# Index rows and one-hots of a token router: one broadcast row and every second one-hot of the first coefficient build move to TensorE and ScalarE

## The chip, the cores and the metric

The kernel runs on one core of a Trainium2 chip. The metric is the device time of one launch in microseconds (us); the time given for a kernel is the median of its runs. Engines are called TensorE (PE in the profile), VectorE (DVE), ScalarE (ACT), GpSimd (POOL) and SyncE (SP, which only issues transfers here).

## The reference, cut to what matters

The network is one hybrid layer; the part that matters is its last block, PEER: 8 heads pick 16 experts each for every token, out of 128 x 128.

```python
idx = ...                                   # (tokens, 128): index = i1 * 128 + i2, 16 for each of 8 heads
u   = jnp.take(u_tab, it, axis=0)           # one 2048-long row per pick
act = jax.nn.gelu(jnp.einsum("td,tkd->tk", xt, u))
v   = jnp.take(v_tab, it, axis=0)
out = jnp.einsum("tk,tkd->td", gt * act, v)
```

There are 256 tokens, in two tiles of 128 (tile 0 and tile 1), and 128 picks ("slots") per token.

## The kernel before, in words

The dot product of a token with a picked row is split by columns. The last 1280 columns are gathered: `dot` fetches one row per token for one slot (GpSimd, an indirect transfer into one of five `u` buffers) and VectorE multiplies it with the token and sums (L861). The first 768 columns are done densely: `dense` multiplies all 16384 rows with all tokens on TensorE and leaves the products in `W[0]` (tile 0) and `W[1]` (tile 1).

Then the picked products have to be taken out of `W`. This is `settle`, which runs beside the last gathered dots. For each of 32 groups of 4 tokens, `extract` loads the two index rows of the group's 4 x 128 picks, broadcast to all 128 partitions (`ids`, L906; the first index is row 0, the second row 1). From row 1 ScalarE makes a one-hot E (Abs with the partition number as bias, L908, then Relu, L909). TensorE multiplies `W` with it (`y`, L912). `pick` then compares row 0 with the partition number on VectorE and multiplies with y (`hit`, L920), and TensorE sums over the partitions (`more`, L922). `ids` lies in one of five places of 512 columns in tensors that are free by then (`id_at`: two in `hnF`, three in `hnT`); a place is loaded again when its `hit` is done.

After the 32 groups of tile 0 come those of tile 1, and between them `build` for tile 0: for each group of 4 tokens VectorE makes two one-hots R and L (L929), R is scaled by the coefficients (four scalings of 128 columns, L936 on ScalarE or L938 on VectorE, as the string `R_BY` says), TensorE multiplies them (`pw`, L939), and ScalarE copies the result into `W` (L940), which now holds a dense matrix of coefficients. When all dots and picks are done, 32 builds for tile 1 follow without other work beside them. The last stage multiplies the coefficients with all rows of the second table.

The order of VectorE's work is written out by hand: each dot is one tick, and 2.4 steps of `settle` are laid behind each tick. Other engines get their order from a scheduler. The picks start in the row behind tick 185:

```python
R_BY = ('AAAA', 'AVAV')                      # L68: scalings of a build: A = ScalarE, V = VectorE
for n in range(groups + LAG):                # settle, LAG = 2
    if n < groups: held[n] = extract(routes[tt], n)
    if n >= LAG:   pick(routes[tt], n - LAG, *held[n - LAG])
    if tt and n < groups: build(routes[0], n, R_BY[0], "ut", 2)
```

E has two buffers. R, L and `hit` share four (tag "raw"), and `pw` of the first builds uses two PSUM buffers (tag "ut").

Of the kernel before, what the change touches and what calls it, by code (L numbers as in the profile page):

```python
# [9 lines left out]
F32 = mybir.dt.float32  # L10
F32R = mybir.dt.float32r
BF16 = mybir.dt.bfloat16
I32 = mybir.dt.int32
U32 = mybir.dt.uint32
AF = mybir.ActivationFunctionType
ALU = mybir.AluOpType
# [4 lines left out]
P = 128  # L21
T = 256
NTT = T // P
# [15 lines left out]
NSLOT = PH * TOPK  # L39
# [7 lines left out]
KD = 6  # L47
# [17 lines left out]
SETTLE_RATE = 2.4  # L65
SETTLE_AT = 185
LAG = 2
R_BY = ('AAAA', 'AVAV')  # L68


@with_exitstack
def trunk(ctx, tc, a, out, dbg=None):
    nc = tc.nc
    V, S, G, PE, SY = nc.vector, nc.scalar, nc.gpsimd, nc.tensor, nc.sync

    def bc(ap, shape):
        return ap.to_broadcast(shape)
# [3 lines left out]
    dram = ctx.enter_context(tc.tile_pool(name="dram", bufs=1, space=DRAM))  # L81
# [7 lines left out]
    iota = consts.tile([P, T], F32, name="iota")  # L89
# [3 lines left out]
    identb = consts.tile([P, P], BF16, name="identb")  # L93
    V.tensor_copy(identb, ident)
    part = consts.tile([P, 2], F32, name="part")
# [25 lines left out]
    with ExitStack() as wctx:  # L121
        atx = wctx.enter_context(ExitStack())
        wp = wctx.enter_context(tc.tile_pool(name="wp", bufs=3, side="right"))
        at = atx.enter_context(tc.tile_pool(name="at", bufs=1))
# [71 lines left out]
        with ExitStack() as mctx:  # L196
# [165 lines left out]
            for i, nm in enumerate(("ssm_c_re", "ssm_c_im")):  # L362
# [3 lines left out]
                for w in range(2):  # L366
                    V.tensor_scalar(cbd[:, :, w, :], craw, par[:, w:w + 1], -1.0 if i else 1.0, op0=ALU.mult,
                                    op1=ALU.mult)
# [192 lines left out]
            for k in range(CW):  # L561
                for q in range(CQ):
                    src = cpad[:, q, k:k + T]
                    if k == 0:
                        V.tensor_scalar(acc[:, q, :], src, cwT[:, q, 0:1], colv[:, 0, q:q + 1], op0=ALU.mult,
                                        op1=ALU.add)
                    else:
                        V.scalar_tensor_tensor(acc[:, q, :], src, cwT[:, q, k:k + 1], acc[:, q, :],  # L568
                                               op0=ALU.mult, op1=ALU.add)
# [4 lines left out]
            for q in range(CQ):  # L574
                S.activation(acc[:, q, :], acc[:, q, :], AF.Silu, bias=colv[:, 2, q:q + 1],
                             scale=colv[:, 1, q:q + 1])
# [122 lines left out]
        rt = uctx.enter_context(tc.tile_pool(name="rt", bufs=1))  # L699
        up = uctx.enter_context(tc.tile_pool(name="up", bufs=1))  # L700
        gp = uctx.enter_context(tc.tile_pool(name="gp", bufs=GATHER_BUFS))
        hnF = up.tile([P, NTT, DG], F32, name="hnF")
        hnT = up.tile([P, KD, T], F32, name="hnT")
# [29 lines left out]
        for tt in range(NTT):  # L733
            V.tensor_scalar(dg[:, tt, :], ident, r8[:, tt:tt + 1], None, op0=ALU.mult)
            PE.matmul(pr[:, tt * P:(tt + 1) * P], ones, dg[:, tt, :], start=tt == 0, stop=tt == 1,
                      skip_group_check=True)
# [12 lines left out]
    class Route:  # L749
# [70 lines left out]
        def gates(self):  # L820
            self.gate = gate = rt.tile([P, PH, TOPK], F32, name="gate", bufs=2)
            gs = rt.tile([P, 2, PH], F32, name="gs")
            V.tensor_sub(gate, self.tm, bc(self.tm[:, :, 0:1], [P, PH, TOPK]))
            S.activation(gate, gate, AF.Exp)
            ib = rt.tile([P, 2, NSLOT], BF16, name="ib")
            S.copy(ib, self.II.rearrange("p s h k -> p s (h k)"))
            for i in range(4):
                SY.dma_start(ib_dram[self.tt][:, i], ib[i * NQ:(i + 1) * NQ].rearrange("n s k -> n (s k)"))
            for _ in range(6):
                yield  # L830
            V.tensor_reduce(gs[:, 0], gate, axis=AX.X, op=ALU.add)
            V.reciprocal(gs[:, 1], gs[:, 0])
            V.tensor_mul(gate, gate, bc(gs[:, 1, :, None], [P, PH, TOPK]))
            V.tensor_scalar(vidx[self.tt], self.uidx.rearrange("p h k -> p (h k)"), float((DC - DU) // GU), None,
                            op0=ALU.add)
            pt = psu.tile([P, 2, P], F32, name="ptc", tag="pw", bufs=1)
            for i in range(2):
                PE.transpose(pt[:, i, :], self.II[:, i].rearrange("p h k -> p (h k)"), ident)
            self.tr = lr_p.tile([P, 2, P], F32, name="tr", bufs=2)
            S.copy(self.tr, pt)  # L840
            yield
# [14 lines left out]
        def dot(self, j):  # L856
# [5 lines left out]
                                   accum_out=self.act[:, j:j + 1])  # L862

    NQ = P // 4
    id_at = [x.bitcast(BF16).rearrange("p (i s k) -> p i s k", i=4, s=2) for x in
             [hnF[:, 0, n * 512:(n + 1) * 512] for n in range(2)]
             + [hnT.rearrange("p k t -> p (k t)")[:, n * 512:(n + 1) * 512] for n in range(KD // 2)]]
    ib_dram = [dram.tile([NQ, 4, 2 * NSLOT], BF16, name=f"ib_dram{tt}") for tt in range(NTT)]
    coef = [consts.tile([P, NSLOT], F32, name=f"coef{tt}") for tt in range(NTT)]
    vidx = [consts.tile([P, NSLOT], I32, name=f"vidx{tt}") for tt in range(NTT)]  # L870
    wa_p = ctx.enter_context(tc.tile_pool(name="wa_p", bufs=1, side="right", reuse_waits="tile"))
# [1 line left out]
    lr_p = lr_x.enter_context(tc.tile_pool(name="lr_p", bufs=2, side="right", reuse_waits="tile"))  # L873
    psx = ctx.enter_context(ExitStack())
    psu = psx.enter_context(tc.tile_pool(name="psu", bufs=2, space=PSUM))
# [6 lines left out]
    def dense():  # L882
        for b in range(NB):
# [17 lines left out]
                S.copy(W[1][:, b - 1:b + 1, :], ps[:, :, P:])  # L901
            yield

    def extract(route, g):
        ids = id_at[(route.tt * NQ + g) % len(id_at)]
        SY.dma_start(ids.rearrange("p i s k -> p i (s k)"), ib_dram[route.tt][g:g + 1].to_broadcast([P, 4, 2 * NSLOT]))  # L906
        E = lr_p.tile([P, 4, P], F32, name="E", tag="ut", bufs=2)
        S.activation(E, ids[:, :, 1, :], AF.Abs, bias=part[:, 1:2], scale=1.0)  # L908
        S.activation(E, E, AF.Relu, bias=1.0, scale=-1.0)  # L909
        y = psu.tile([P, 4, P], F32, name="y", tag=("sy", "sy", "pw")[g % 3], bufs=(2, 2, 1)[g % 3])  # L910
        for i in range(4):
            PE.matmul(y[:, i, :], W[1][:, :, i * NQ + g] if route.tt else W[0][:, i * NQ + g, :], E[:, i, :], start=i == 0, stop=i == 3,  # L912
                      skip_group_check=True)
        return ids, y

    def pick(route, g, ids, y):
        if g == 0:
            route.more = psu.tile([P, NSLOT], F32, name="more", bufs=1)
        hit = lr_p.tile([P, 4, P], F32, name="hit", tag="raw", bufs=4)
        V.scalar_tensor_tensor(hit, ids[:, :, 0, :], part[:, 0:1], y, op0=ALU.is_equal, op1=ALU.mult)  # L920
        for i in range(4):
            PE.matmul(route.more[i * NQ:(i + 1) * NQ, :], onecol[:, NQ - g:2 * NQ - g], hit[:, i, :], start=g == 0,  # L922
                      stop=g == NQ - 1)

    def build(route, g, by, tag, bufs):
        ts = slice(4 * g, 4 * g + 4)
        LR = [lr_p.tile([P, 4, P], F32, name=nm, tag="raw", bufs=4) for nm in "RL"]
        for x, at in zip(LR, (0, 1)):
            V.tensor_tensor(x, bc(iota[:, None, :P], [P, 4, P]), bc(route.tr[:, at, ts, None], [P, 4, P]),  # L929
                            op=ALU.is_equal)  # L930
        R, L = LR
        pw = psu.tile([P, 4, P], F32, name="pw", tag=tag, bufs=bufs)
        for i in range(4):
            c = route.cT[:, 4 * g + i:4 * g + i + 1]
            if by[i] == "A":
                S.activation(R[:, i, :], R[:, i, :], AF.Copy, scale=c)  # L936
            else:
                V.tensor_scalar(R[:, i, :], R[:, i, :], c, None, op0=ALU.mult)  # L938
            PE.matmul(pw[:, i, :], L[:, i, :], R[:, i, :], start=i == 0, stop=i == 3, skip_group_check=True)  # L939
        S.copy(W[route.tt][:, :, ts], pw.rearrange("p t b -> p b t"))  # L940
# [29 lines left out]
    def settle():  # L970
        groups = P // 4
        for tt in range(NTT):
            held = {}
            for n in range(groups + LAG):
                if n < groups:
                    held[n] = extract(routes[tt], n)
                    yield
                if n >= LAG:
                    pick(routes[tt], n - LAG, *held[n - LAG])
                    yield  # L980
                if tt and n < groups:
                    build(routes[0], n, R_BY[0], "ut", 2)
                    yield
            if tt == 0:
                while tick[0] <= NSLOT:
                    yield
                yield from routes[0].finish()
# [10 lines left out]
    for tt in range(NTT):  # L998
        for g in range(len(GROUPS[tt])):
            while (tt, g) not in ready:  # L1000
                next(routing)
            h0, n = routes[tt].heads(g)
# [13 lines left out]
    for g in range(P // 4):  # L1016
        build(routes[1], g, R_BY[1], ("sy", "ut")[g % 2], 2)
    uctx.close()
# [68 lines left out]
    for tt, st in enumerate(sts):  # L1087
        for c, cs_ in enumerate([slice(DC, D)] + COLS):
# [4 lines left out]
            else:  # L1093
                V.scalar_tensor_tensor(sq[tt][:, cs_], src, st[:, NCH + 2:NCH + 3], gF[:, cs_], op0=ALU.mult,
                                       op1=ALU.mult)
# [30 lines left out]
```

## Time and profile before

| what | value |
|---|---|
| median of 3 runs | 2144.23 us (2141.84 to 2145.15) |
| the profiled execution: its time, its span | 2139.49 us, 2137.6 us |
| busy share of the span | PE 92%, DVE 83%, ACT 47%, POOL 34% |
| picks of tile 0 (first `hit` to the last) | 1340.8 to 1413.2 us |
| picks of tile 1 with the builds of tile 0 | 1417.8 to 1545.7 us |
| builds of tile 1 | 1549.9 to 1602.3 us |

The shares are averages over all stages. A stage is read from its own window: which engine is busy through it, and who waits for whom.

### The profile page before, as it was taken

What the parts mean: (1) busy time and instruction counts of PE and PEld (TensorE: products, weight loads), DVE (VectorE), ACT (ScalarE), POOL (GpSimd) and SP (SyncE); (2) the same over time, 40 slices, a digit from 0 to 9 for tenths busy, and PEclk for the clock granted to TensorE, in tenths of its full rate; (3) what the DMA queues carried; (4) which work ended last, traced back from release to release, by engine and by line L of the source; (5) the groups of instructions that cost most, each with busy time, mean ns of one, the idle gap of its engine ahead of it and who ended that gap; (6) DMA issues with size and microseconds to landing.
All of it is one profiled execution on the core that took longest, in us unless ns stands there. A gap on an engine that the chain in (4) does not pass through costs nothing.

```text
span 2137.6 us, 31790 instructions
## 1 busy us (share of the span) xinstructions
PE 1970.1 (92%) x11459; PEld 1699.6 (80%) x11459; DVE 1776.7 (83%) x2903; ACT 1002.5 (47%) x1681; POOL 736.9 (34%) x546
## 2 busy tenths in 40 slices
PE   8998888999999999899999998689779999999997
PEld 7987786677799888788878886567667888888886
DVE  6789999987665557999976666889998899899997
ACT  5764444446444445233333333467673444444444
POOL 0000000000000003444455666433207777677773
PEclk9999899999999999999999999789899999999998
DMA  7554444554965567789999999988619999999995
GB/s 251 161 180 151 127 150 133 163 172 148 313 204 169 166 201 275 268 308 343 319 345 401 404 408 380 363 315 273 204 68 314 359 350 339 343 337 340 340 338 197
DMA packets 199132, 567.59 MB, mean 266 GB/s; under 512 B 31537, under 2 KB 36513, under 8 KB 198848
## 3 DMA queue, kind: packets, MB, share of 16 engines
q1 hardware_dynamic: 141632, 322.27, 45.7%
q0 software_dynamic: 57344, 243.30, 30.2%
q8 instruction: 90, 1.47, 0.3%
q14 instruction: 66, 0.54, 0.1%
HBM read 553.57 MB, written 11.93 MB: 265 GB/s over the span
## 4 chain that ended last, share of the span: by engine, by line
PE 47%; DVE 23%; issue 12%; DMA 9%; POOL 6%; ACT 3%; SPq 0%; POOLq 0%; DVEq 0%; ACTq 0%
PE acc L1073 8%; PE acc L1074 8%; PE acc L1072 8%; POOL u L859 5%; DVE u L861 5%; PE mm L183 4%; PE mm L181 4%; PE mm L182 4%; DVE acc L568 3%; DVE w_lo L163 3%; DMA hnT<-ib_dram 2%; PE mm L173 2%; PE mm L174 2%; PE mm L172 2%; DMA hnF<-ib_dram 1%
## 5 line engine op out<-in xcount | busy, mean ns | idle before, releaser
L861 DVE SCALAR_TENSOR_TENSOR u<-u,hnF 128x1280 f32<-128x1280 f32 x256 | 388.5, 1520 | 86.5 <-DMA u<-in_peer_u,uidx 84.9
L1037 POOL DMA_INDIRECT v<-in_peer_v,vidx x256 | 383.8, 1499 | 190.2 <-ACT WB L940 68.8
L859 POOL DMA_INDIRECT u<-in_peer_u,uidx x256 | 311.2, 1216 | 338.7 <-DVE u L861 262.9
L162 ACT CAST w_hi<-w_raw 128x1024 fp32r<-128x1024 f32 (+2 forms) x228 | 231.4, 1017 | 289.7 <-PE mm L182 125.0
L163 DVE TENSOR_TENSOR w_lo<-w_raw,w_hi 128x1024 fp32r<-128x1024 f32 (+2 forms) x228 | 277.2, 1219 | 106.9 <-ACT w_hi L162 103.1
L897 PE MATMUL sy<-hnT,ut 128*128 128x256 f32 x1536 | 356.8, 385 | 9.3 <-ACT ut L893 9.3
L897 PEld LDWEIGHTS sy<-hnT,ut 128*128 128x128 f32 x1536 | 287.1, 193 | 50.5 <-ACT ut L893 15.1
L103 ACT CAST vh<-vr 128x1472 fp32r<-128x1472 f32 x128 | 183.2, 1431 | 263.6 <-PE acc L1073 263.6
L1073 PE MATMUL acc<-vh,wl 128*128 128x512 f32 (+1 forms) x768 | 296.9, 387 | 3.6 <-DVE wl L1063 3.6
L183 PE MATMUL mm<-aT_hi,w_lo 128*128 128x256 f32 x960 | 274.3, 295 | 26.7 <-DVE w_lo L163 26.5
L1074 PE MATMUL acc<-vl,wh 128*128 128x512 f32 (+1 forms) x768 | 295.2, 386 | 0.0
L742 POOL TENSOR_TENSOR hnT<-aT_hi,aT_lo 128x1024 f32<-128x1024 f32 (+1 forms) x2 | 3.8, 1904 | 812.9 <-ACT w_hi L162 812.9
L181 PE MATMUL mm<-aT_hi,w_hi 128*128 128x256 f32 x960 | 279.8, 294 | 3.7 <-DVE sg L264 2.3
L1072 PE MATMUL acc<-vh,wh 128*128 128x512 f32 (+1 forms) x768 | 277.1, 385 | 2.7 <-ACT vh L103 2.2
L182 PE MATMUL mm<-aT_lo,w_hi 128*128 128x256 f32 x960 | 276.9, 291 | 0.0
L104 DVE TENSOR_TENSOR vl<-vr,vh 128x1472 fp32r<-128x1472 f32 x128 | 216.6, 1692 | 38.3 <-ACT vh L103 38.0
L1039 DVE SCALAR_TENSOR_TENSOR accg<-v,coef,accg 128x576 f32<-128x576 f32 x256 | 208.9, 816 | 11.9 <-DMA v<-in_peer_v,vidx 8.1
L183 PEld LDWEIGHTS mm<-aT_hi,w_lo 128*128 128x128 f32 x960 | 186.4, 198 | 34.3 <-DVE w_lo L163 30.6
L181 PEld LDWEIGHTS mm<-aT_hi,w_hi 128*128 128x128 f32 x960 | 189.3, 198 | 7.8 <-DVE sg L264 2.5
L182 PEld LDWEIGHTS mm<-aT_lo,w_hi 128*128 128x128 f32 x960 | 189.8, 198 | 1.3 <-issue 0.4
L893 ACT COPY ut<-ut 128x768 f32<-128x768 f32 x128 | 100.3, 801 | 165.6 <-PE ut L891 163.1
L1073 PEld LDWEIGHTS acc<-vh,wl 128*128 128x128 f32 x768 | 145.2, 189 | 35.0 <-DVE wl L1063 4.7
(333 smaller groups left out, 3362.7 us busy)
## 6 DMA issues: line engine op xcount, KB each, us to landing
vr<-in_peer_v SPq DMA_DIRECT2D x128, 736.0 KB, 6.7
raw<-in_peer_u SPq DMA_DIRECT2D x128, 384.0 KB, 6.4
w_raw<-in_w_kv_mem SPq DMA_DIRECT2D x64, 512.0 KB, 3.8
w_raw<-in_w_in SPq DMA_DIRECT2D x48, 512.0 KB, 4.0
w_raw<-in_w_out SPq DMA_DIRECT2D x32, 512.0 KB, 5.4
w_raw<-in_w_q_mem SPq DMA_DIRECT2D x32, 512.0 KB, 4.3
w_raw<-in_w_o_mem SPq DMA_DIRECT2D x32, 512.0 KB, 4.6
hnT<-ib_dram SPq DMA_DIRECT2D x38, 256.0 KB, 5.8
```

What stands on the lines that cost most here:

```text
L162: S.copy(hi, raw)
L163: V.tensor_sub(lo, raw, hi.bitcast(F32))
L181: PE.matmul(o, wh, ah, start=first and cb % 2 == 0, stop=False, skip_group_check=True)
L182: PE.matmul(o, wh, al, start=False, stop=False, skip_group_check=True)
L183: PE.matmul(o, wl, ah, start=False, stop=last and end, skip_group_check=True)
L859: G.indirect_dma_start(out=u, out_offset=None, in_=a["peer_u"].rearrange("e (q c) -> (e q) c", c=GU), in_offset=bass.IndirectOffsetOnAxis( ...
L861: V.scalar_tensor_tensor(u, u, 1.0, hnF[:, self.tt, :], op0=ALU.mult, op1=ALU.mult, accum_out=self.act[:, j:j + 1])
L897: PE.matmul(ps[:, b % 2, :], ut[:, k, :], hnT[:, k, :], start=k == 0 and b % 2 == 0, stop=k == KD - 1 and b % 2 == 1, skip_group_check=True)
L1037: G.indirect_dma_start(out=v, out_offset=None, in_=table, in_offset=bass.IndirectOffsetOnAxis(ap=vidx[tt][:, j:j + 1], axis=0))
L1072: PE.matmul(o, wh[:, tt, :], vh[:, cs_], start=b == 0, stop=False)
L1073: PE.matmul(o, wl[:, tt, :], vh[:, cs_], start=False, stop=False)
L1074: PE.matmul(o, wh[:, tt, :], vl[:, cs_], start=False, stop=b == NB - 1)
```

## The change: what it does

Three things are changed.

- Tile 0's `extract` loads only index row 0. Row 1 is put on all partitions by TensorE: four matmuls whose weights are one column of the identity, broadcast, and whose moving operand is `ib` (the bf16 index rows, now kept). ScalarE reads the result from PSUM (`pb`). A place is half as wide for tile 0, so there are eleven instead of five; tile 1 has five as before.
- In the builds of tile 0 every second group (g odd, `far`) gets its one-hot R from two bf16 matmuls into PSUM (`df`: index minus column number), and ScalarE's Abs and Relu; L stays on VectorE.
- In the builds of tile 1 ScalarE does three of the four scalings and VectorE one (`AAVA`).

```diff
-R_BY = ('AAAA', 'AVAV')
+R_BY = ('AAAA', 'AAVA')
...
-            ib = rt.tile([P, 2, NSLOT], BF16, name="ib")
+            self.ib = ib = rt.tile([P, 2, NSLOT], BF16, name="ib", bufs=2)
...
+    def id_tiles(ns):
+        n = ns * 2 * P
+        room = [hnF[:, 0, :], hnT.rearrange("p k t -> p (k t)")]
+        return [x[:, i:i + n].bitcast(BF16).rearrange("p (s i k) -> p s i k", i=4, s=ns) for x in room
+                for i in range(0, x.shape[1] - n + 1, n)]
+
+    id_at = [id_tiles(1), id_tiles(2)]
...
+    row0 = lr_p.tile([P, P], BF16, name="row0", bufs=1)
+    G.memset(row0, 0.0)
+    G.memset(row0[0:1, :], 1.0)
+    falling = lr_p.tile([P, P], BF16, name="falling", bufs=1)
+    S.activation(falling, iota[:, :P], AF.Copy, scale=-1.0)
...
-        S.activation(E, ids[:, :, 1, :], AF.Abs, bias=part[:, 1:2], scale=1.0)
+        if route.tt:
+            at = ids[:, 1]
+        else:
+            at = psu.tile([P, 4, P], F32, name="pb", tag="ut")
+            for i in range(4):
+                t = i * NQ + g
+                PE.matmul(at[:, i, :], bc(identb[:, t:t + 1], [P, P]), route.ib[:, 1, :], start=i == 0, stop=i == 3,
+                          skip_group_check=True)
+        S.activation(E, at, AF.Abs, bias=part[:, 1:2], scale=1.0)
...
-        for x, at in zip(LR, (0, 1)):
+        far = route.tt == 0 and g % 2 == 1
+        if far:
+            df = psu.tile([P, 4, P], F32, name="df", tag="ut")
+            PE.matmul(df, route.ib[:, 0, :], bc(identb[:, ts, None], [P, 4, P]), start=True, stop=False)
+            PE.matmul(df, row0, bc(falling[:, None, :], [P, 4, P]), start=False, stop=True)
+            S.activation(LR[0], df, AF.Abs)
+            S.activation(LR[0], LR[0], AF.Relu, bias=1.0, scale=-1.0)
+        for x, at in list(zip(LR, (0, 1)))[far:]:
```

How the instructions stand now, at three places. On SP's queue the index loads of tile 0 (`ib_dram_8319`) stood, before, in runs of two and three; `hnF` and `hnT` are the tensors in which the places lie:

```order
L906 DMA hnF<-ib_dram_8319 128x1024 x2
L906 DMA hnT<-ib_dram_8319 128x1024 x3
L906 DMA hnF<-ib_dram_8319 128x1024 x2
L906 DMA hnT<-ib_dram_8319 128x1024 x3
L906 DMA hnF<-ib_dram_8319 128x1024 x2
```

In the change they stand in runs of five and six at half the width, and the first two-row loads of tile 1 (`ib_dram_8320`) follow:

```order
L917 DMA hnF<-ib_dram_8319 128x512 x5
L917 DMA hnT<-ib_dram_8319 128x512 x6
L917 DMA hnF<-ib_dram_8319 128x512 x5
L917 DMA hnT<-ib_dram_8319 128x512 x6
L917 DMA hnF<-ib_dram_8319 128x512 x5
L917 DMA hnT<-ib_dram_8319 128x512 x5
L917 DMA hnF<-ib_dram_8320 128x1024 x2
L917 DMA hnT<-ib_dram_8320 128x1024 x3
```

The load of a place thus stands eleven groups ahead of its use instead of five.

On ScalarE, in the middle of tile 1's picks, two builds of tile 0 stood like this before (E: the one-hot of a pick, R: a build's scalings, WA: the copy of a finished build):

```order
L936 ACTIVATE R<-R,cT 128x128 x4
L908 ACTIVATE E<-hnT,part 128x512
L909 ACTIVATE E<-E 128x512
L936 ACTIVATE R<-R,cT 128x128 x4
L908 ACTIVATE E<-hnF,part 128x512
L940 COPY WA<-pw 128x128x4
L909 ACTIVATE E<-E 128x512
L940 COPY WA<-pw 128x128x4
```

In the change, for two builds of which the first is `far`:

```order
L953 ACTIVATE R<-df 128x512
L928 ACTIVATE E<-hnF,part 128x512
L954 ACTIVATE R<-R 128x512
L929 ACTIVATE E<-E 128x512
L963 ACTIVATE R<-R,cT 128x128 x4
L928 ACTIVATE E<-hnF,part 128x512
L929 ACTIVATE E<-E 128x512
L963 ACTIVATE R<-R,cT 128x128 x4
L967 COPY WA<-pw 128x128x4
L928 ACTIVATE E<-hnT,part 128x512
L967 COPY WA<-pw 128x128x4
```

The Abs and Relu of R are new, and between them and the copy that frees a PSUM buffer stand two E that wait for index loads.

On TensorE, at the same place, before:

```order
L922 MATMUL more<-hit,onecol 32x128 x4
L912 MATMUL y<-E,WB 128x128 x4
L939 MATMUL pw<-R,L 128x128 x4
L922 MATMUL more<-hit,onecol 32x128 x4
L912 MATMUL y<-E,WB 128x128 x4
L939 MATMUL pw<-R,L 128x128 x4
```

and in the change:

```order
L951 MATMUL df<-identb,ib 128x512
L952 LDWEIGHTS row_8338
L952 MATMUL df<-falling,row_8338 128x512
L942 MATMUL more<-hit,onecol 32x128 x4
L932 MATMUL y<-E,WB 128x128 x4
L942 MATMUL more<-hit,onecol 32x128 x4
L932 MATMUL y<-E,WB 128x128 x4
L966 MATMUL pw<-R,L 128x128 x8
```

The matmuls of two builds now stand together behind two y, and the `df` of the next pair directly behind them.

## Rows read from the trace of the kernel before

**Rows 1.** Busy time by stage (windows); PEclk is TensorE's granted clock, then DMA share, GB/s.

```profile
core 0: us, PE busy (x) PEld busy (x) DVE busy (x) ACT busy (x) POOL busy (x), PEclk, DMA share, GB/s
1340.80:1413.20 72.40, 54.76 (x488) 40.99 (x489) 59.50 (x87) 37.61 (x57) 28.05 (x27) 0.81 0.97 357
...
1417.80:1545.70 127.90, 112.00 (x757) 96.93 (x755) 118.92 (x181) 92.36 (x218) 39.01 (x38) 0.94 0.76 253
...
1549.90:1602.30 52.40, 38.08 (x256) 33.26 (x256) 49.02 (x124) 37.56 (x97) 0.00 (x0) 0.95 0.20 70
1602.30:2120.00 517.70, 512.08 (x2289) 432.69 (x2290) 465.21 (x640) 234.24 (x386) 383.75 (x256) 0.99 0.92 332
```

**Rows 2.** Waits, 1340.8 to 1413.2: total us, times, longest.

```profile
ACT E L908 <- DMA hnF<-ib_dram: 20.9, 10, 13.0
...
ACT E L908 <- DMA hnT<-ib_dram: 13.6, 12, 1.9
DVE hit L920 <- PE y L912: 11.0, 15, 2.8
...
DVE u L861 <- DMA u<-in_peer_u,uidx: 1.8, 2, 1.6
```

**Rows 3.** Transfers, 1340.8 to 1413.2: queues; issues, size, us to landing.

```profile
q0 software_dynamic: 3960, 18.02, 65.3%
q1 hardware_dynamic: 4253, 7.76, 31.6%
...
hnT<-ib_dram SPq DMA_DIRECT2D x18, 256.0 KB, 7.3
...
u<-in_peer_u,uidx POOLq DMA_INDIRECT x27, 7.7
```

**Rows 4.** TensorE in order of time (start, us), second stage, where nothing stalls it.

```profile
1447.85 0.43 PE L922 MATMUL more<-hit,onecol 128*32 128x128 f32 x8
1448.20 2.02 PE L912 MATMUL y<-E,WB 128*128 128x128 f32 x8
1450.05 1.06 PE L939 MATMUL pw<-R,L 128*128 128x128 f32 x8
1451.04 0.43 PE L922 MATMUL more<-hit,onecol 128*32 128x128 f32 x8
```

**Rows 5.** VectorE in order of time, second stage.

```profile
1535.98 0.69 DVE L929 TENSOR_TENSOR L<-iota,tr 128x512 f32<-128x512 f32 x1
1536.58 1.49 DVE L861 SCALAR_TENSOR_TENSOR u<-u,hnF 128x1280 f32<-128x1280 f32 x1
...
1537.99 0.75 DVE L920 SCALAR_TENSOR_TENSOR hit<-hnF,part,y 128x512 f32<-128x512 bf16 x1
```

**Rows 6.** ScalarE's groups, 1417.8 to 1545.7: busy, mean ns, idle before.

```profile
L936 ACT ACTIVATE R<-R,cT 128x128 f32<-128x128 f32 x128 | 40.6, 389 | 0.5 <-DVE R L929 0.5
L940 ACT COPY WA<-pw 128x512 f32<-128x512 f32 x32 | 18.6, 582 | 15.8 <-PE pw L939 15.4
L909 ACT ACTIVATE E<-E 128x512 f32<-128x512 f32 x29 | 18.2, 626 | 0.4
L908 ACT ACTIVATE E<-hnT,part 128x512 f32<-128x512 bf16 x17 | 12.3, 722 | 9.9 <-DMA hnT<-ib_dram 9.8
L908 ACT ACTIVATE E<-hnF,part 128x512 f32<-128x512 bf16 x12 | 8.7, 721 | 6.7 <-DMA hnF<-ib_dram 5.1 <-PE y L912 1.6
```

**Rows 7.** VectorE and ScalarE in order of time, builds of tile 1.

```profile
1562.38 0.68 DVE L929 TENSOR_TENSOR R<-iota,tr 128x512 f32<-128x512 f32 x1
...
1563.10 0.69 ACT L936 ACTIVATE R<-R,cT 128x128 f32<-128x128 f32 x2 [0.43 <-DVE R L929]
1563.59 0.48 DVE L938 TENSOR_SCALAR R<-R,cT 128x128 f32<-128x128 f32 x2
1563.70 0.56 ACT L940 COPY WB<-pw 128x512 f32<-128x512 f32 x1
...
1563.98 0.69 DVE L929 TENSOR_TENSOR R<-iota,tr 128x512 f32<-128x512 f32 x1
...
1564.70 0.69 ACT L936 ACTIVATE R<-R,cT 128x128 f32<-128x128 f32 x2 [0.44 <-DVE R L929]
```

More of the change, by code (lines that the diff above doesn't have):

```diff
@@ L824, in gates @@
             S.activation(gate, gate, AF.Exp)
-            ib = rt.tile([P, 2, NSLOT], BF16, name="ib")
+            self.ib = ib = rt.tile([P, 2, NSLOT], BF16, name="ib", bufs=2)
             S.copy(ib, self.II.rearrange("p s h k -> p s (h k)"))
             for i in range(4):
-                SY.dma_start(ib_dram[self.tt][:, i], ib[i * NQ:(i + 1) * NQ].rearrange("n s k -> n (s k)"))
+                SY.dma_start(ib_dram[self.tt][:, :, i], ib[i * NQ:(i + 1) * NQ])
             for _ in range(6):
@@ L864, in trunk @@
     NQ = P // 4
[L865 to L868, printed above, removed]
+    def id_tiles(ns):
[4 more added lines that the diff above has]
+    id_at = [id_tiles(1), id_tiles(2)]
+    ib_dram = [dram.tile([NQ, 2, 4, NSLOT], BF16, name=f"ib_dram{tt}") for tt in range(NTT)]
     coef = [consts.tile([P, NSLOT], F32, name=f"coef{tt}") for tt in range(NTT)]
@@ L902, in dense @@
             yield
+    row0 = lr_p.tile([P, P], BF16, name="row0", bufs=1)
[3 more added lines that the diff above has]
+    S.activation(falling, iota[:, :P], AF.Copy, scale=-1.0)
     def extract(route, g):
-        ids = id_at[(route.tt * NQ + g) % len(id_at)]
-        SY.dma_start(ids.rearrange("p i s k -> p i (s k)"), ib_dram[route.tt][g:g + 1].to_broadcast([P, 4, 2 * NSLOT]))
+        ids = id_at[route.tt][g % len(id_at[route.tt])]
+        ns = 1 + route.tt
+        SY.dma_start(ids.rearrange("p s i k -> p s (i k)"),
+                     ib_dram[route.tt][g:g + 1, :ns].rearrange("n s i k -> n s (i k)").to_broadcast([P, ns, 4 * NSLOT]))
         E = lr_p.tile([P, 4, P], F32, name="E", tag="ut", bufs=2)
-        S.activation(E, ids[:, :, 1, :], AF.Abs, bias=part[:, 1:2], scale=1.0)
+        if route.tt:
[7 more added lines that the diff above has]
+        S.activation(E, at, AF.Abs, bias=part[:, 1:2], scale=1.0)
         S.activation(E, E, AF.Relu, bias=1.0, scale=-1.0)
@@ L919, in pick @@
         hit = lr_p.tile([P, 4, P], F32, name="hit", tag="raw", bufs=4)
-        V.scalar_tensor_tensor(hit, ids[:, :, 0, :], part[:, 0:1], y, op0=ALU.is_equal, op1=ALU.mult)
+        V.scalar_tensor_tensor(hit, ids[:, 0], part[:, 0:1], y, op0=ALU.is_equal, op1=ALU.mult)
         for i in range(4):
```

## The prediction

> **What bounds the kernel now.** I read the busy time by stage first, since the shares over the whole span mix stages. Three stages are touched, and the last one, the product with the second table, is not: there TensorE is busy 512.1 of 517.7 us, and it can't start before the builds of tile 1 are done, since each of its products needs coefficients of all tokens [rows 1]. So every microsecond by which the builds end earlier or later moves the end of the kernel by as much.
>
> First stage, picks of tile 0: 72.4 us. VectorE is busy for 59.5 of it, while the transfers have a share of 0.97 and TensorE's granted clock is 0.81, a mix of its two levels [rows 1]. The waits tell the order of things: VectorE waits 11.0 us for y, and ScalarE, which makes the one-hot that y needs, waits 20.9 + 13.6 = 34.5 us for index rows [rows 2]. These are 256 KB each and land 7.3 us after issue, in the middle of 27 gathers [rows 3]. The index rows end last here.
>
> Second stage, picks of tile 1 and builds of tile 0: 127.9 us, VectorE 118.9, TensorE 112.0, ScalarE 92.4 [rows 1]. VectorE bounds it, with 9.0 us of idle time.
>
> Third stage, builds of tile 1: one build every 1.60 us (from R to R), and VectorE runs without a gap while ScalarE stands idle for 0.44 us of each [rows 7].
>
> **First stage, priced.** Removed: ScalarE's wait for index rows, and half the bytes of 32 broadcasts. Moved: the loads stand eleven places ahead, and only `hit` needs them. Three things can bound the stage afterwards.
> - VectorE: 59.5 us, unchanged [rows 1].
> - Transfers: the gathers' queue took 65.3% of the 16 engines' time, 47.3 us; the other 31.6%, 22.9 us, for 7.76 MB, which is 30 broadcasts of 262 KB or 0.77 us each [rows 3]. Of tile 0's 32 rows 11 now land before the first `hit`; 21 remain, and I count four of tile 1's. A half row costs 0.38 us if bytes set the price, 0.77 if the number of packets does (it stays at 128). So 47.3 + 4 x 0.77 + 21 x 0.38 to 0.77 = 58.4 to 66.6 us.
> - TensorE: the new `pb` are four loads of weights and four matmuls of 128 columns a group. No bf16 matmul of this shape is in the trace. Above stands half of a `pw` of 8 instructions with 128-column weights (from 1450.05 to 1451.04: 0.99, half is 0.5), below half of a `more` with 32-column weights (0.35, half is 0.18) [rows 4]; I take 0.4, since the weights are as wide as those of `pw`. 32 x 0.4 = 13 us. At the clock of 0.81 that makes 54.8 + 13 / 0.81 = 70.8 us; if the clock rises to the second stage's 0.94 [rows 1], 54.8 x 0.81 / 0.94 + 13 / 0.94 = 61 us. It should rise, since TensorE has fewer waits, but not at once.
>
> I take 65 us, the middle of TensorE's two cases: 7.4 us gained. The bounds are 61 (VectorE's 59.5 and its 1.8 us of waits for gathers [rows 2]) and 70.8, so 11.4 to 1.6. What is late next is y, by TensorE instead of by the index rows.
>
> **Second stage, priced.** VectorE loses 16 one-hots of 0.60 us each (L to the next instruction, 1535.98 to 1536.58 [rows 5]): 118.9 - 9.6 = 109.3. ScalarE gains 16 times an Abs out of PSUM and a Relu. The nearest rows are a copy out of PSUM of the same size (0.58), the Abs of E (0.72) and its Relu (0.63) [rows 6]: between 1.21 and 1.35 for both; I take 1.2, since neighbours overlap by a little: 92.4 + 19.2 = 111.6. TensorE gains 16 `df`, two matmuls of 512 columns with two loads of weights. They stream 1024 columns as a `more` does (0.35 for eight times 128), and at most cost as a `pw` (0.99) [rows 4]; I take 0.5, nearer to the first, since there are two loads of weights instead of eight. TensorE's own cycle without stalls is 3.19 us (more to more, 1447.85 to 1451.04 [rows 4]): 32 x 3.19 + 8 = 110.
>
> So three engines come to 109 to 112 us each where one had 119. In a chain of in-order queues that feed each other, equal loads cost more waiting, not less: on ScalarE each E that waits for its index row now holds up the Abs, Relu and scalings behind it, for which `pw` waits on TensorE. Before, the longest engine had 9.0 us of idle time; I add a third and take 12: 124 us, 3.9 gained. The bounds are 116 (half of the idle time, all else hidden) and 136 (the third rival): 11.9 gained to 8.3 lost.
>
> **Third stage, priced.** ScalarE has two scalings (0.30 us apart, 0.69 for both), the copy, and the gap. One more scaling of 0.30 fits into the gap of 0.44, so ScalarE comes to 1.60 - 0.44 + 0.30 = 1.46; VectorE loses one of two scalings that take 0.39 (1563.59 to 1563.98): 1.60 - 0.19 = 1.41 [rows 7]. The period becomes 1.46: 32 x 0.14 = 4.5 us. The first builds are paced by the coefficients' arrival, so I take 4.0, with bounds of 3 and 5.
>
> **At nothing:** `row0` and `falling` are made once, beside the dense loop, in which ScalarE and GpSimd wait; exposed they would cost under 1 us (a 128-column ScalarE instruction takes 0.39 [rows 6]). The writes of `ib_dram` are as many as before and are read much later.
>
> **Sum.** 7.4 + 3.9 + 4.0 = 15.3. The profiled execution took 2139.5 us, 4.7 below the median of the runs shown; the same difference on the median gives 2144.2 - 15.3 = 2129 us.
>
> **Rivals.**
> 1. The first stage stays bound by transfers or by TensorE's low clock. For it: a share of 0.97 and a clock of 0.81 [rows 1]. Against it: fewer bytes. 70.8 us there: 1.6 + 3.9 + 4.0 = 9.5 gained, 2135 us. The Trainium skill (DMA: Bandwidth & Descriptors, Specifications) gives 512 B as the smallest transfer at line rate, so rows of 1 KB should cost by their bytes; no run here shows such a row yet.
> 2. The second stage follows VectorE after all, 116 us: 7.4 + 11.9 + 4.0 = 23.3, 2121 us. For it: ScalarE had 33.3 us idle there, the sum of its groups' idle times [rows 6].
> 3. `df` takes a PSUM buffer that is free only when ScalarE has copied a `pw`, and that copy stands behind E's that wait for index rows, 9.9 + 6.7 = 16.6 us in the stage [rows 6]. Half of that falls into the stretch of a `far` build; if it comes on top, the stage takes 127.9 + 8.3 = 136 us, and 7.4 - 8.3 + 4.0 = 3.1 gained: 2141 us, no change that can be measured.
> 4. Slower: ScalarE's queue becomes the chain of the second stage. If its waits stay as they are, since they are waits for others (92.4 + 33.3 = 125.7 [rows 1, 6]), and each `far` adds its full 1.35, the stage takes 125.7 + 21.6 = 147 us, 19.4 more; with the other two terms 8.0 lost, 2152 us. It decides from 1.0 us uncovered per `far` build ((11.4 + 4.3) / 16). Against it: 15.4 us of these waits are for `pw`, which waits for R, and would shrink with it. The one-hot takes ScalarE about twice VectorE's time (1.35 against 0.69 [rows 5, 6]). That is the rule of the Trainium skill (ScalarE: Activation LUTs, Rules for kernel authors): Relu and its like belong on VectorE, not on ScalarE. Here the trace agrees on the price of one instruction; by the rule alone the move would cost time.
>
> **How the numbers follow.** My forecast 0.55, rival 1 0.15, rival 2 0.12, rival 3 0.11, rival 4 0.07. 0.2% (4.3 us) is about what a measurement of this kernel tells from no change. Forecast and rivals 1 and 2 are faster: 0.82; rival 3 the same: 0.11; rival 4 slower: 0.07. The range leaves out the last two, 0.18: it goes from 2117 (all three terms near their best: 11.4 + 11.9 + 4.0 = 27) to 2140.
>
> **What would show it.** E of tile 0 no longer waits for any transfer; its first stage takes about 65 us with TensorE's clock above 0.81 (70 and a DMA share near 1: rival 1). The second stage takes about 124 us with ScalarE busy about 111; idle time before `df` and behind E's waits would speak for rival 3, ScalarE without gaps for rival 4. The builds of tile 1 come every 1.46 us. I am wrong if the second stage grows by more than 11 us, or if the last stage takes longer than its 518 us.

## The result

The changed kernel takes 2124.52 us (median of 4 runs, 2121.98 to 2127.19), the kernel before 2144.23: a ratio of 0.9915, with a 95% interval of 0.9899 to 0.993. That is 19.7 us less where 15.3 were forecast. The profiled execution took 2121.98 us (span 2120.0), 17.5 less than that of before. One kernel further down (`hit`'s buffers alone) had two slow runs among its five, 3160.74 and 3809.32 us, which stand in no ratio here.

Busy time by stage after the change (windows; columns as in [rows 1]): picks of tile 0, picks of tile 1 with builds of tile 0, builds of tile 1, and the last stage.

```profile
1342.30:1402.80 60.50, 53.41 (x597) 41.99 (x597) 58.24 (x87) 39.60 (x59) 25.75 (x28) 0.96 0.97 363
...
1406.40:1532.60 126.20, 113.85 (x784) 94.57 (x784) 110.00 (x163) 106.81 (x250) 39.08 (x38) 0.97 0.78 258
...
1536.80:1583.50 46.70, 37.74 (x256) 32.84 (x256) 42.66 (x92) 45.26 (x130) 0.34 (x1) 0.95 0.23 78
1583.50:2102.00 518.50, 511.56 (x2287) 432.48 (x2288) 465.61 (x640) 234.17 (x387) 385.36 (x256) 0.99 0.93 332
```

Against [rows 1] the first stage is 11.9 us shorter (7.4 forecast), the second 1.7 (3.9), the third 5.7 (4.0). The last stage lasts as long as before, within 1 us. The first `hit` came 1.5 us later: over the fourteen executions profiled here it lies anywhere from 1337.5 to 1347.9 us, in the ten with half-size rows from 1341.7 on, in the four others up to 1341.9. The 1.5 us are there already at the first gathered dot, some 500 us earlier (844.4 us before, 845.9 after; 843.1 to 851.3 over the fourteen); whether the rest of the spread belongs to the half rows stays open. So the length of a stage says more than one run's total.

**First stage.** Waits of the changed kernel, 1342.3 to 1402.8 (total us, times, longest), to be read beside [rows 2]:

```profile
ACT E L928 <- PE y L932: 29.1, 24, 15.7
...
DVE u L861 <- DMA u<-in_peer_u,uidx: 1.5, 3, 0.5
```

E's waits for index rows, 34.5 us, are gone, and so are VectorE's 11.0 for y. ScalarE's 29.1 us are harmless: it is ahead and waits until y has read an older E. VectorE is busy for 58.24 of the 60.50 us, so the stage now lasts as long as VectorE's own work. The transfers of the same stretch, beside [rows 3] (packets, MB, share of 16 engines):

```profile
q0 software_dynamic: 4010, 18.26, 77.0%
q1 hardware_dynamic: 3495, 3.62, 19.4%
```

The engines are as full as before (0.97), since the stage shrank as its transfers did: the index rows take 11.7 us of the 16 engines where they took 22.9, the gathers 46.6 where they took 47.3. VectorE hardly waits for them (1.5 us above), so the transfers are close behind VectorE and do not end last. TensorE's clock, cut at the middle of the stage:

```profile
1342.30:1372.50 30.20, 26.68 (x294) 21.12 (x295) 28.71 (x44) 18.47 (x28) 13.06 (x14) 0.92 0.98 369
1372.50:1402.80 30.30, 26.73 (x306) 20.87 (x304) 29.52 (x44) 21.13 (x31) 12.69 (x14) 1.00 0.96 358
```

The granted clock was 0.81 over this stage before; it is 0.92 in the first half and 1.00 in the second, so nearly all of the stage runs at the upper of the two levels. TensorE stands idle for less of it: 53.41 of 60.50 us busy, 54.76 of 72.40 before. A `pb` in order of time:

```profile
1375.56 1.16 PE L932 MATMUL y<-E,WA 128*128 128x128 f32 x8
1376.55 0.39 PE L926 MATMUL pb<-ib,identb 128*128 128x128 bf16 x4
1376.87 0.32 PE L942 MATMUL more<-hit,onecol 128*32 128x128 f32 x4
```

0.32 us from `pb` to the next instruction, where 0.4 was taken.

**Second stage.** VectorE lost 8.9 us of work (118.92 to 110.00), as forecast, and gained 7.2 of idle time: 9.0 us became 16.2. Its waits, and TensorE's for the scalings, 1406.4 to 1532.6:

```profile
PE pw L966 <- ACT R L963: 8.2, 14, 1.1
DVE L L956 <- PE more L942: 7.3, 7, 1.5
...
DVE L L956 <- PE pw L966: 5.4, 6, 1.2
...
DVE hit L940 <- PE pw L966: 3.2, 8, 1.1
```

A one-hot that waits for `more`, and a `hit` that waits for `pw`, wait for nothing that they read: `hit`, R and L share four SBUF buffers, so a one-hot takes one that a `hit` had, and `hit` one that a one-hot had. VectorE in order of time:

```profile
1465.32 0.74 DVE L940 SCALAR_TENSOR_TENSOR hit<-hnT,part,y 128x512 f32<-128x512 bf16 x1
1465.98 0.68 DVE L956 TENSOR_TENSOR R<-iota,tr 128x512 f32<-128x512 f32 x1
1468.19 0.69 DVE L956 TENSOR_TENSOR L<-iota,tr 128x512 f32<-128x512 f32 x1 [1.52 <-PE more L942]
```

VectorE stands still for 1.52 us after R, with all of L's inputs there, until `more` has read the `hit` of 1465.32.

**Third stage.** VectorE and ScalarE in order of time, beside [rows 7]:

```profile
1560.73 0.68 DVE L956 TENSOR_TENSOR R<-iota,tr 128x512 f32<-128x512 f32 x1
...
1560.94 0.56 ACT L967 COPY WB<-pw 128x512 f32<-128x512 f32 x1
...
1561.45 0.98 ACT L963 ACTIVATE R<-R,cT 128x128 f32<-128x128 f32 x3
1561.93 0.28 DVE L965 TENSOR_SCALAR R<-R,cT 128x128 f32<-128x128 f32 x1
1562.13 0.68 DVE L956 TENSOR_TENSOR R<-iota,tr 128x512 f32<-128x512 f32 x1
...
1562.34 0.56 ACT L967 COPY WB<-pw 128x512 f32<-128x512 f32 x1
```

One build every 1.40 us (1562.13 - 1560.73) where 1.46 was forecast, with no gap on either engine: the scalings follow the copy after 0.51 us, not after its full 0.56.

### The profile page after: what moved, and what is told of

It is laid out like the page before. It is cut to its first block, busy times and chain, and to the rows that moved or that the text cites. A ratio compares the mean times of both kernels' runs of the same rounds, so it can differ in the third digit from the quotient of the medians.

```text
span 2120.0 us, 32032 instructions
## 1 busy us (share of the span) xinstructions
PE 1970.8 (93%) x11619; PEld 1698.4 (80%) x11619; DVE 1760.7 (83%) x2855; ACT 1024.5 (48%) x1746; POOL 736.2 (35%) x548
## 3 DMA queue, kind: packets, MB, share of 16 engines
q1 hardware_dynamic: 141888, 318.08, 45.5%
## 4 chain that ended last, share of the span: by engine, by line
PE 48%; DVE 25%; issue 13%; POOL 6%; DMA 5%; ACT 2%; SPq 0%; DVEq 0%; POOLq 0%; ACTq 0%
PE acc L1100 8%; PE acc L1101 8%; PE acc L1099 8%; DVE u L861 6%; POOL u L859 5%; PE mm L183 4%; PE mm L181 4%; PE mm L182 4%; DVE acc L568 3%; DVE w_lo L163 3%; PE mm L174 2%; PE mm L173 2%; PE mm L172 2%; PE y L932 1%; DMA hnT<-ib_dram 1%
## 5 line engine op out<-in xcount | busy, mean ns | idle before, releaser
L163 DVE TENSOR_TENSOR w_lo<-w_raw,w_hi 128x1024 fp32r<-128x1024 f32 (+2 forms) x228 | 270.8, 1190 | 111.5 <-ACT w_hi L162 111.3
L901 PEld LDWEIGHTS sy<-hnT,ut 128*128 128x128 f32 x1536 | 287.3, 193 | 48.6 <-ACT ut L897 11.9
```

What stands on the lines that cost most here:

```text
L163: V.tensor_sub(lo, raw, hi.bitcast(F32))
L901: PE.matmul(ps[:, b % 2, :], ut[:, k, :], hnT[:, k, :], start=k == 0 and b % 2 == 0, stop=k == KD - 1 and b % 2 == 1, skip_group_check=True)
```

## The experiments

Each is compared with runs of the kernel before on the same chip; differences in us are to their median. In this section stages are cut at marks in the program, so that kernels compare: the first from the first `hit` to the add that ends tile 0's picks, the second from the first scaling of tile 0's builds to the add that ends tile 1's picks, the third from the first scaling of tile 1 to the start of the last copy but one. The kernel before has 72.4, 128.7 and 50.5 by these marks, the changed one 60.4, 127.9 and 45.1. Their second stages:

```profile
1419.39:1548.08 128.69, 110.42 (x749) 95.34 (x748) 119.71 (x181) 91.73 (x218) 38.13 (x37) 0.94 0.76 250
```

```profile
1407.17:1535.04 127.87, 113.08 (x782) 93.80 (x781) 111.67 (x166) 106.81 (x250) 38.31 (x38) 0.97 0.77 252
```

### The parts alone

**The picks alone.** The changed kernel with

```diff
-R_BY = ('AAAA', 'AAVA')
+R_BY = ('AAAA', 'AVAV')
...
-        far = route.tt == 0 and g % 2 == 1
+        far = False
```

> The first part alone: one index row of tile 0 made by TensorE, half-size loads, eleven places; both one-hots of every build are VectorE's again and tile 1's scalings alternate again. Theory (the three parts add up, stage by stage): the first stage takes 60.5 us as in the changed kernel, the second 127.9 and the third 52.4 as before, the first hit comes 1.5 later: 12 - 1.5 = 10.5 us less than before, about 2134. Rival (the one-hots moved away from VectorE in the second stage let the first stage end earlier, or the picks of tile 1 also gain from the loads' new form): less than 7 or more than 13 us gained, with the second stage away from 127.9 by over 2.

2133.16 us against 2145.83, 12.7 less; ratio 0.9934 (0.9915 to 0.9952). The first stage took 60.0 us, the second 128.7, the third 50.4. The rival is out: the other parts have no share in the first stage. Behind it stands 1.8 us that was not foreseen: from the add to the first scaling 4.4 us instead of 6.2.

**The one-hots alone.** The kernel before with `row0`, `falling`, the lines on `far` in `build`, and

```diff
-            ib = rt.tile([P, 2, NSLOT], BF16, name="ib")
+            self.ib = ib = rt.tile([P, 2, NSLOT], BF16, name="ib", bufs=2)
```

> The second part alone: in the kernel before, every second right one-hot of tile 0's builds is made by TensorE and ScalarE; loads, places and scalings are those of before. Theory (the second stage's cycle runs over TensorE, ScalarE and VectorE in turn, so 8.9 us less of VectorE's work mostly turns into its waits): 1 to 3 us less than before, about 2142, with VectorE busy 110 and idle 16 of the second stage's 126. Rival A (the part gains its full 8.9 us alone, and the other parts took it back): about 2135. Rival B (ScalarE's queue pays for it, and the 1.7 us of the changed kernel came from the other parts): slower than before by 1 us or more.

2142.81 us against 2145.83, 3.0 less; ratio 0.9981 (0.9968 to 0.9994). The total is what the theory said, the stage is not:

```profile
1421.02:1553.47 132.45, 115.56 (x781) 96.17 (x780) 110.47 (x164) 106.11 (x250) 38.22 (x37) 0.93 0.76 242
```

VectorE has 22 us of idle time here, and the stage is 3.8 us longer than before. The profiled execution (2145.08 us) lies near the top of its twelve times (2138.04 to 2146.38), so total and trace don't fit well. What holds is that 9 us of work taken from VectorE gave far less than 9 us.

**The scalings alone.** The kernel before with the one line of `R_BY`.

> The third part alone: in the kernel before, three of four scalings of tile 1's builds are ScalarE's instead of two. Theory: the builds come every 1.40 us instead of 1.60, as in the changed kernel: 5.6 us less than before, about 2138.6. Rival (the first builds of the stage had been held by something that the other parts removed): 4 us or less.

2138.29 us against 2145.83, 7.5 less; ratio 0.9968 (0.9954 to 0.9983). Third stage:

```profile
1549.40:1594.92 45.52, 37.16 (x249) 32.61 (x250) 42.76 (x92) 44.28 (x126) 0.00 (x0) 0.93 0.23 80
```

45.5 us instead of 50.5: 5.0 in the stage, inside the interval of the total. This part stands by itself.

**All but the one-hots.** The changed kernel with `far = False`.

> The changed kernel without its second part: both one-hots of every build are VectorE's, all else as changed. Theory (the one-hots on ScalarE are worth 1.7 us): 15.8 to 16.5 us less than before, so about 1.7 slower than the changed kernel, with the second stage at 128. Rival (they are worth nothing or cost something, and the second stage shrank for another reason): as fast as the changed kernel or faster, 17.5 us or more below before.

2124.75 us against 2145.83, 21.1 less; ratio 0.9898 (0.9879 to 0.9918), beside 0.9915 for the whole change. The second stage took 128.9 us, 1.0 more than with them. By the times the rival is right: in this change the one-hots are worth nothing that can be measured.

### What the first stage was waiting for

**Five places.**

```diff
-    id_at = [id_tiles(1), id_tiles(2)]
+    id_at = [id_tiles(1)[:5], id_tiles(2)]
```

> The changed kernel with five index places of half size for tile 0 instead of eleven. Theory (only hit needs the row now, two groups later than E did, and five groups of 1.85 us cover the 7.3 us of a load; six rows more fall into the stage): first stage 60.5 to 63 us, total 0 to 2 us above the changed kernel. Rival (the depth is what ends the stall): first stage 66 us or more, with hit waiting for its transfer, total 5 us or more above the changed kernel.

2127.47 us against 2142.45, 15.0 less; ratio 0.9933 (0.9914 to 0.9952). The first stage is 58.8 us, so depth isn't what ended its stall. The second is 132.0, 4.1 more than in the change, which neither theory had. Its row, and the first E of tile 1 on ScalarE, of the change and then of this kernel:

```profile
1404.97:1536.98 132.01, 118.49 (x800) 99.82 (x800) 111.49 (x166) 110.28 (x256) 38.32 (x38) 0.95 0.76 245
```

```profile
1396.71 0.72 ACT L928 ACTIVATE E<-hnF,part 128x512 f32<-128x512 bf16 x1 [0.72 <-PE y L932]
...
1404.94 0.72 ACT L928 ACTIVATE E<-hnT,part 128x512 f32<-128x512 bf16 x1
```

```profile
1406.15 1.32 ACT L928 ACTIVATE E<-hnF,part 128x512 f32<-128x512 bf16 x2
```

In the change three E of tile 1 start before the first scaling (1407.17), the first at 1396.71 and the third at 1404.94; here the first starts 1.2 us behind it (1404.97). So 800 instead of 782 of TensorE's instructions and 256 instead of 250 of ScalarE's fall into the stage. With eleven places `hnF` is free of tile 0's rows earlier: its first two loads for tile 1 are issued at 1386.8 and 1391.0 us in the change, here at 1395.8 and 1399.2. That this is the whole of the 4 us was not tried.

**Both rows.** Five places of full size and `ns = 2`: the row for E is loaded again, and not used.

> The changed kernel with both index rows of tile 0 loaded again (full-size loads, five places as before), though the one for E is not used: TensorE still makes it. It separates the bytes from E's independence. Theory A (bytes: the 16 DMA engines are full through the stage, so each of 27 loads costs 0.77 us beside 47 us of gathers): first stage 68 to 72 us, total 8 us or more above the changed kernel. Theory B (independence: E no longer waits, and the transfers only shift in time): first stage 60 to 63 us, total within 3 us of the changed kernel.

2138.39 us against 2142.45, 4.1 less; ratio 0.9981 (0.9966 to 0.9996). The first stage lies between the theories:

```profile
1340.08:1405.76 65.68, 53.45 (x588) 40.90 (x588) 59.02 (x87) 36.89 (x55) 25.24 (x27) 0.94 1.02 396
```

Of the 12 us, E's independence gives 6.7 (72.4 to 65.7), and half the bytes 5 to 7 (65.7 to 60.4, or to 58.8 with five places). These are single traces: the unchanged first stage took 72.4, 73.5 and 74.2 us in three, and the execution profiled here (2132.81 us) is among the fastest of its twelve (2129.65 to 2142.69). The second stage took 134.3 us, again with the first E of tile 1 behind the first scaling, as with five half places. The index rows' queue here, and with five half places (58.8 us):

```profile
q1 hardware_dynamic: 4175, 7.62, 31.5%
```

```profile
q1 hardware_dynamic: 4014, 3.78, 20.0%
```

20.7 us of the 16 engines against 11.8, for half the bytes and 4% fewer packets: a half row costs 0.57 of a full one, between the two bounds and nearer to bytes. The Trainium skill (DMA: Bandwidth & Descriptors, Specifications) has line rate from 512 B on, which would make it 0.50 for these 1 KB rows (an estimate); the trace comes near to it, and the measured 0.57 decides.

### What holds the second stage

**Both buffer rules.** The changed kernel with

```diff
-        hit = lr_p.tile([P, 4, P], F32, name="hit", tag="raw", bufs=4)
+        hit = lr_p.tile([P, 4, P], F32, name="hit", tag="hit" if route.tt else "raw", bufs=2 if route.tt else 4)
...
-            df = psu.tile([P, 4, P], F32, name="df", tag="ut")
+            dp = psu.tile([P, 2, 4, P], F32, name="dp", tag="ut")
+            df = dp[:, 0]
...
-        pw = psu.tile([P, 4, P], F32, name="pw", tag=tag, bufs=bufs)
+        pw = dp[:, 1] if far else psu.tile([P, 4, P], F32, name="pw", tag=tag, bufs=bufs)
```

> The changed kernel with two buffer rules of the second stage altered: hit of tile 1 has two SBUF buffers of its own, so that R and L share four with each other alone, and df and the pw of the same build lie in one PSUM buffer of two banks, so that df waits for the copy of the build before last and not of the last one. Theory (VectorE's 16 us of idle time in the second stage are waits for buffers: one-hots for more and pw, df for a copy): the second stage falls from 127.9 to 118 to 122, total 6 to 10 us below the changed kernel. Rival (the idle time is a chain through R's scalings on ScalarE, and buffers only show where it ends): second stage 126 or more, total within 2 us of the changed kernel.

2111.52 us against 2142.45, 30.9 less; ratio 0.9855 (0.9835 to 0.9876).

```profile
1410.51:1525.49 114.98, 108.42 (x783) 92.10 (x782) 110.35 (x166) 105.14 (x250) 37.87 (x38) 0.98 0.81 281
```

The stage falls by 12.9 us, more than expected, and VectorE's idle time from 16.2 to 4.6. The chain through the scalings was no cause of its own.

**df beside pw alone.** The last two hunks without the first.

> The changed kernel with df and the pw of the same build in one PSUM buffer of two banks; hit shares its SBUF buffers as in the change. Theory (it is hit's SBUF buffers that hold the second stage, since VectorE waits there for more 7.3 and pw 8.6 us and nowhere for df): second stage 125 to 128 us, total 0 to 3 us below the changed kernel, about 2123. Rival (df's wait for ScalarE's copy of the last pw, the third rival of the prediction, is what keeps the stage long): second stage 120 or less, total 7 us or more below the changed kernel.

2126.93 us against 2142.06, 15.1 less; ratio 0.9921 (0.9907 to 0.9935), no better than the change. Second stage 129.5 us, a little above the theory's band, and far from the rival's.

**hit's buffers alone.** The first hunk without the others.

> The changed kernel with two SBUF buffers of its own for hit of tile 1; df takes its PSUM buffer as in the change. Theory (hit's buffers hold the stage): second stage 115 to 119 us, total 9 to 13 us below the changed kernel, about 2113. Rival (df's PSUM buffer): second stage 124 or more, total 4 us below the changed kernel at most. If both are needed, each of the two runs gains less than 4 us.

2112.53 us against 2142.06; ratio 0.9854 (0.9834 to 0.9874), the same as with both rules. Its second stage, and VectorE's only wait of weight in it:

```profile
1408.06:1523.74 115.68, 108.48 (x783) 92.40 (x781) 110.46 (x166) 105.32 (x250) 37.87 (x38) 0.99 0.82 280
```

```profile
DVE L L956 <- PE pw L966: 4.2, 8, 0.7
```

The waits of L for `more` and of `hit` for `pw` are gone. The buffers of `hit` were the cause, and `df`'s place in PSUM was not. Whether six buffers shared by all three tiles would do as well was not tried.

**hit's buffers, all one-hots on VectorE.** The first hunk and `far = False`.

> The changed kernel without its second part (all one-hots on VectorE) and with two buffers of its own for hit of tile 1. Theory (VectorE is busy 120 of 129 us there and its one-hots wait for buffers): second stage 124 to 126 us, total 3 to 5 us below the kernel without the second part alone. Rival (VectorE's idle time there comes from elsewhere): second stage 128 or more, total within 2 us of that kernel. Beside the run with both it shows what one-hots on TensorE and ScalarE are worth where buffers don't bind: 4 to 5 us by the theory.

2113.09 us against 2142.45; ratio 0.9863 (0.9844 to 0.9883). Second stage:

```profile
1409.63:1533.01 123.38, 108.32 (x750) 93.74 (x749) 119.55 (x181) 91.42 (x218) 38.30 (x38) 0.93 0.79 262
```

The stage comes out near the theory's 124 to 126, and the gain on the kernel without the one-hots alone is larger than expected (0.9863 against 0.9898). The profiled execution took 2119.38 us, the other three about 2113, so trace and total don't fit well; the same kernel a second time:

> The kernel with hit's own buffers and all one-hots on VectorE once more, since its profiled execution (second stage 123.4 us) was 6 us above its three other times, and those were as fast as with half of the one-hots on TensorE and ScalarE. Theory (with the buffers out of the way VectorE's work sets the stage, so the one-hots moved are worth 5 us or more): second stage 121 to 125 us, ratio to before 0.988 or more. Rival (VectorE has no idle time left to win either way and the moved one-hots are worth 2 us or less): second stage 119 or less, ratio 0.987 or less.

2118.14 us against 2145.06; ratio 0.988 (0.9864 to 0.9896).

```profile
1410.69:1531.82 121.13, 107.47 (x750) 93.45 (x749) 119.75 (x181) 91.78 (x218) 38.38 (x38) 0.96 0.80 267
```

With buffers of its own for `hit`, the one-hots on TensorE and ScalarE shorten the stage by 5.4 to 8.4 us (121.1 and 123.4 against 115.0 and 115.7). In the totals they are worth 2 us (0.9863 against 0.9855, 0.8 thousandths) to 5.5 (0.988 against 0.9854), and the intervals touch: by the stage they pay, by the total it is likely and no more.

**All right one-hots moved.** Both buffer rules, and

```diff
-        far = route.tt == 0 and g % 2 == 1
+        far = route.tt == 0
```

> The version with both buffer rules, with every right one-hot of tile 0's builds made by TensorE and ScalarE instead of every second. Theory (with the buffers out of the way the longest engine sets the stage): ScalarE comes to 105 + 16 x 1.2 = 124 us of work and VectorE to 101, so the second stage takes 126 to 130 us, total 11 to 15 us above the version with half of them, about 2125. Rival (VectorE's work sets the stage even so): 110 us or less, total 4 us or more below it.

2124.3 us against 2142.06, 17.8 less; ratio 0.9914 (0.9898 to 0.993), 12.6 us (0.0059) above the version with half of them.

```profile
1403.91:1535.95 132.04, 119.23 (x812) 97.58 (x812) 104.17 (x153) 121.40 (x281) 37.24 (x38) 0.97 0.74 250
```

```profile
DVE L L957 <- PE dp L967: 27.9, 26, 2.5
```

The stage is 2 us above what the theory had at most. ScalarE (121.4) is now the longest and VectorE waits 27.9 us for `pw`, which needs ScalarE's scalings. That fits the fourth rival's mechanism, reached with twice the one-hots; what the other 10.6 us of the stage are was not taken apart. Of none, half and all, half is the best in the stage.

## Why the prediction was right, and where its sizes were off

The time, 2124.5, lies in the range, between the forecast (2129) and the second rival (2121). The first and the third part gained in their stages and by the wait and the work named for them; the second took the work off VectorE and gained next to nothing. What bounds the first stage afterwards and why the second gained so little were named wrongly, and that the sum is off by only 4.4 us is in part luck: the stages were off by +4.5, -2.2 and +1.7. Step by step:

- **First stage, 11.9 us for 7.4.** The step that was mis-sized is "I take 65 us, the middle of TensorE's two cases". The granted clock went to 0.92 and then 1.00, a `pb` took 0.32 us for 0.4, and TensorE was busy for 53.4 us where its two cases had 61 and 70.8. So "what is late next is y" failed: VectorE's waits for y are gone, and its own 58.2 us of work end last, the prediction's lower bound (61, measured 60.5). That TensorE's better case gives 61 as well is chance. The transfers came to 58.7 us (0.97 of 60.5), near the lower end of 58.4 to 66.6. Rival 1 is out: its 70.8 us did not come, and the DMA share stayed near 1 because the stage shrank with the bytes.
- **Second stage, 1.7 us for 3.9.** The terms of work hold: VectorE lost 8.9 us (9.6 taken), TensorE came to 113.9 (110), ScalarE to 106.8 (111.6). Two rows of the change price the new work of ScalarE (mean ns):

```profile
L954 ACT ACTIVATE R<-R 128x512 f32<-128x512 f32 x16 | 10.0, 627 | 0.0
L953 ACT ACTIVATE R<-df 128x512 f32<-128x512 f32 x16 | 9.7, 603 | 0.0
```

  Together 1.23 us, in the bounds of 1.21 to 1.35. On the queue they add less, since neighbours overlap: ScalarE's busy time grew by 14.4 us (92.36 to 106.81), 0.90 us a pair where 1.2 was taken. What failed is the reason for the idle time: "in a chain of in-order queues that feed each other, equal loads cost more waiting". With two more buffers the same loads, as equal as before, wait 5 us instead of 16. The waits were for the buffers that `hit` shares with R and L. They stand in the trace of before too, and the prediction did not read them (VectorE's waits in the second stage of before):

```profile
DVE L L929 <- PE pw L939: 6.3, 9, 1.7
DVE L L929 <- PE more L922: 1.8, 2, 1.5
DVE hit L920 <- PE pw L939: 0.8, 2, 0.5
```

  None of the three is for an operand; together they are 8.9 of VectorE's 9.0 us of idle time. So the buffers cost time already, without any moved one-hot: in the changed kernel with all one-hots on VectorE, `hit`'s own buffers took the stage from 128.9 to 123.4 and 121.1 us. VectorE, with 9 us less to do, came to these buffers earlier and stood there longer (15.9 us).
- **Rival 2**, 2121 us, is near the total by chance: the second stage did not follow VectorE in the change. It does as soon as `hit` has its own buffers, to 115 us, even a little below the rival's 116.
- **Rival 3** is out: `df`'s buffer costs nothing that can be seen (129.5 us with `df` beside `pw`, 127.9 without).
- **Rival 4** did not occur. The Trainium skill (ScalarE: Activation LUTs, Rules for kernel authors) would keep Relu on VectorE. The trace agrees that the moved one-hot is the dearer one, 1.23 us for 0.69, and in the change as it stands the move gains nothing; but where VectorE ends last and ScalarE has room, the stage shortens by 5.4 to 8.4 us, against the rule.
- **Third stage, 5.7 us for 4.0.** The step is ScalarE's 1.46 us per build: its copy's last 0.05 us lie under the next scaling. So both engines come to 1.40.

## What to carry to other kernels

Before work is moved off the busiest engine, look at what this engine's idle time waits for: a wait for an instruction whose result isn't read is a wait for a buffer, and what is taken off the engine turns into more of it. Buffers that tiles of two chains share tie the chains together; two more, for `hit` alone (4 KB of each partition), were worth 10 to 13 us on top of the change, and only with them did the moved one-hots shorten their stage. A DMA share near 1 does not say that the same bytes need the whole stage: with both rows loaded it went from 72.4 to 65.7 us, at shares of 0.97 and 1.02. Only the 5 to 7 us below that came from fewer bytes.

## Not expected of the hardware

TensorE's granted clock in the first stage went from 0.81 to 0.96 although the kernel gave it more instructions (597 matmuls for 488) in less time; before, it stood idle for 17.6 us of that stage, now for 7.1. And index rows of half the size took 0.57 of the engines' time, not 0.50.
